# One output piece a block whose low part comes from an accumulating DMA, and eight instead of five blocks a feed-forward sum by all seven products

## The chip, the cores and the metric

The kernel runs on one core of one Trainium2 chip. The core has engines that run side by side, each with its own queue of instructions: TensorE (PE, matmuls; its weight loads are shown as PEld), VectorE (DVE), ScalarE (ACT), GpSimd (POOL) and SyncE (SP). Here SP only issues DMAs; POOL issues DMAs too. The metric is the device time of one execution in microseconds, as the median of several runs. The kernel before took 2389.01 us (three runs, 2388.84 to 2389.03).

## What is computed

One decoder layer in float32, for 256 tokens of width 2048, cut to what matters here:

```python
h = layer_norm(ALPHA * h + 0.5 * swiglu(h, ffn1_w_in, ffn1_w_out), ln1_g, ln1_b)
...
h = layer_norm(ALPHA * h + merged @ w_out, ln2_g, ln2_b)
h = layer_norm(ALPHA * h + 0.5 * swiglu(h, ffn2_w_in, ffn2_w_out), ln3_g, ln3_b)

def swiglu(h, w_in, w_out):
    a, b = split(h @ w_in, 2)
    return (silu(a) * b) @ w_out
```

Between the two feed-forward halves stand attention and a recurrent branch, which form `merged`. The hidden width of a feed-forward half is 5632.

## The kernel before

**Three matmuls for one product.** Each float32 operand is split into a high part, rounded to the format that TensorE streams (`float32r`), and a low part, the rest. A product is high x high + high x low + low x high (`three`, L622 to L625). The weights come from DRAM unsplit, once each, in *pieces* of 128 x 1024 numbers (512 KB), in an order that is fixed while the program is traced (`pieces`, L324 to L380). For each piece ScalarE copies the high part (`wh`, L217) and VectorE subtracts it from the raw weights (`wl`, L218).

**The loop over pieces.** `Weights.unit` (L224) hands TensorE the columns of the current piece, `cur`. At each change of piece it has the loads written down to piece `cur + 8` (AHEAD + LOADS) and the splits to `cur + 4` (AHEAD), and lets every background task go one step (`on_piece`). Plain pieces are loaded to four `raw` buffers; splits have five buffers each for `wh` and `wl` (HL_BUFS).

**Blocks.** The first product of a feed-forward half runs over 22 blocks of 256 hidden columns (a and b, so 512 weight columns). Of a block, the contraction over 2048 is cut into four *chunks* of 512. A chunk is done in one of two ways: as two plain pieces ("c", eight products of the halves of tokens and columns), or by Strassen's scheme with seven products, as four forms of a 1 MB chunk in an `rf` buffer (two such buffers): "p1q3", "p2", "q5p7", "q4p6" (L690 to L704). For the forms VectorE also makes sums of quarters of the weights (`operand`, L182 to L200) before it makes their low parts. Blocks 0 and 1 have no chunk by seven products, block 2 two, later ones three (chunks 1, 2, 3), and the blocks named in FOUR (L96) all four.

**Fills.** Pieces of the second product ("o", output pieces, `fill`, L949) are mixed into the blocks: two in blocks 2 to 5, four in blocks 6 to 21, three of these ahead of the forms and one among them (`block_plan`, L69 to L93). So a three-chunk block has 18 pieces with the last output piece at number 13, counted from 0, and a four-chunk block 20 with the last at number 11. Four output pieces complete 256 tokens x 512 columns for four blocks' hidden columns; the sum goes from PSUM through ScalarE to a `yd` tile and by an accumulating DMA of POOL's to Y (L957 to L961). Y, eight tiles of 128 x 512, is the residual; it is in SBUF during the whole sum. At the end of a block, `gate` (L913) joins the products, applies silu and multiplies.

**After the sums** `out_product` (L871) does the last output pieces, adds the products to Y (`y_add`, L754) and starts the norm, whose power is taken on POOL (L768).

**Buffers and order.** Most tiles of 128 x 512 share the 53 buffers of tag "u" (U_BUFS). A second pool, which `share` (L386) closes and opens again between stages, holds four tiles of forms during the sums ("s") or eight small tiles "t" in the other stages ("t"). The orders of PE, SP and POOL are as the program is written (`manual_schedule`, L293); those of VectorE and ScalarE are made by a planner, which goes by the order of writing and by when it reckons the operands to be there.

## Time and profile before

| | us |
|---|---|
| median of three runs | 2389.01 |
| the profiled execution | 2390.11 |
| its span, first to last instruction | 2388.3 |
| TensorE busy | 2364.0 |
| VectorE busy | 2213.3 |
| ScalarE busy | 1502.0 |
| POOL busy | 123.1 |

The granted TensorE clock was 0.998 of full speed over the span. The profile gives instructions by engine: start, duration, line of the program, operation, output and input tiles with their numbers left out (`wl<-raw,wh`), shapes, and in brackets for how long the engine had been idle before it and what ended that. "DMA to landing" is the time from the issue of a DMA to its last byte. A matmul's duration in the profile is longer than the distance to the next one's start, since matmuls are pipelined; the distance is what counts for time.

The first half runs from the start to about 710 us, of which blocks 0 to 21 to 671, and the second from about 1700 to the end.

### The profile page before, as it was taken

To read this page: it belongs to the slowest core of one execution; us is meant where nothing else is said; L and a number is where in the kernel's file an instruction comes from. 1 tells how busy PE (TensorE), PEld (TensorE's weight loads), DVE (VectorE), ACT (ScalarE), POOL (GpSimd) and SP (SyncE) were. 2 spreads that over 40 slices of the span, in tenths; PEclk is the share of its full clock that TensorE was granted. 3 is DMA by queue.
4 is the path that set the end of the run, shared out by engine and by line. 5 is a ranking of instruction groups with operands and counts; after the bars stand their busy time and mean duration, and the time that the engine had idled before them with its cause. 6 is when DMAs were issued, how large, how long until landed. Compare 5 with 4: busy or idle time off the path is not lost.

```text
span 2388.3 us, 38774 instructions
## 1 busy us (share of the span) xinstructions
PE 2364.0 (99%) x14890; PEld 2111.6 (88%) x14890; DVE 2213.3 (93%) x3127; ACT 1502.0 (63%) x2042; POOL 123.1 (5%) x196
## 2 busy tenths in 40 slices
PE   8999999999999999999999999999999999999997
PEld 6898999989988888888999998888898899899996
DVE  7999999999999998789788888998999999999997
ACT  7666666666647554665588885555766666666662
POOL 0000000000000000001000001100000000000000
PEclk9999999999999999999999999999999999999999
DMA  8666666666666455547655568755675666666665
GB/s 293 193 222 213 227 212 217 219 217 212 195 210 221 177 186 179 187 142 265 207 183 185 187 191 295 252 194 175 209 229 212 221 212 188 230 227 212 216 208 176
DMA packets 123018, 501.24 MB, mean 210 GB/s; under 512 B 14256, under 2 KB 14256, under 8 KB 101968
## 3 DMA queue, kind: packets, MB, share of 16 engines
q1 hardware_dynamic: 104256, 454.60, 54.6%
q0 software_dynamic: 18576, 44.17, 8.1%
q8 instruction: 116, 1.90, 0.3%
q14 instruction: 70, 0.57, 0.1%
HBM read 467.26 MB, written 10.49 MB: 200 GB/s over the span
## 4 chain that ended last, share of the span: by engine, by line
PE 92%; DVE 5%; issue 1%; DMA 1%; ACT 0%; SPq 0%; POOL 0%; DVEq 0%; ACTq 0%; POOLq 0%
PE mm L625 20%; PE mm L623 20%; PE mm L624 20%; PE bp L624 6%; PE bp L623 6%; PE bp L625 6%; PE mm L1248 4%; PE mm L1249 4%; PE mm L1247 4%; DVE wl L218 2%; PE bp L939 1%; DVE ws L190 0%; ACT wh L217 0%; DMA raw<-f1a 0%; PE bp L1128 0%
## 5 line engine op out<-in xcount | busy, mean ns | idle before, releaser
L217 ACT ACTIVATE wh<-raw 128x1024 fp32r<-128x1024 f32 (+2 forms) x540 | 552.3, 1044 | 293.3 <-PE mm L625 169.0
L218 DVE TENSOR_TENSOR wl<-raw,wh 128x1024 fp32r<-128x1024 f32 (+2 forms) x540 | 637.2, 1196 | 96.4 <-ACT wh L217 94.7
L217 ACT ACTIVATE wh<-rf 128x1024 fp32r<-128x1024 f32 (+1 forms) x489 | 439.9, 915 | 313.6 <-PE mm L625 157.3
L218 DVE TENSOR_TENSOR wl<-rf,wh 128x1024 fp32r<-128x1024 f32 (+1 forms) x489 | 505.5, 1040 | 12.8 <-ACT wh L217 7.1
L623 PE MATMUL mm<-wh,hs 128*128 128x512 f32 (+1 forms) x884 | 317.0, 359 | 0.0
L625 PE MATMUL mm<-wh,hs 128*128 128x512 f32 (+1 forms) x884 | 311.1, 352 | 1.1 <-DVE hs L804 1.1
L624 PE MATMUL mm<-wl,hs 128*128 128x512 f32 (+1 forms) x884 | 310.8, 352 | 0.2 <-DVE wl L218 0.2
L625 PE MATMUL mm<-wh,g 128*128 128x512 f32 x704 | 278.2, 395 | 0.2 <-DVE g L747 0.2
L623 PE MATMUL mm<-wh,g 128*128 128x512 f32 x704 | 278.2, 395 | 0.0
L624 PE MATMUL mm<-wl,g 128*128 128x512 f32 x704 | 278.1, 395 | 0.0
L217 ACT ACTIVATE wh<-ws 128x1024 fp32r<-128x1024 f32 x163 | 173.0, 1061 | 141.9 <-PE mm L625 83.9
L623 PE MATMUL bp<-wh,sh 128*128 128x256 f32 x918 | 258.7, 282 | 0.0
L624 PE MATMUL bp<-wl,sh 128*128 128x256 f32 x918 | 256.4, 279 | 1.2 <-DVE wl L218 1.2
L625 PE MATMUL bp<-wh,sl 128*128 128x256 f32 x918 | 256.2, 279 | 0.0
L190 DVE TENSOR_TENSOR ws<-rf 128x1024 f32<-128x1024 f32 x163 | 198.4, 1217 | 7.0 <-DMA rf<-f1a 1.4
L218 DVE TENSOR_TENSOR wl<-ws,wh 128x1024 fp32r<-128x1024 f32 x163 | 198.2, 1216 | 2.8 <-ACT wh L217 2.4
L625 PEld LDWEIGHTS mm<-wh,hs 128*128 128x128 f32 x884 | 165.9, 188 | 27.5 <-DVE hs L804 2.5
L623 PEld LDWEIGHTS mm<-wh,hs 128*128 128x128 f32 x884 | 166.1, 188 | 24.3 <-issue 1.3
L624 PEld LDWEIGHTS mm<-wl,hs 128*128 128x128 f32 x884 | 166.1, 188 | 22.4 <-DVE wl L218 0.7
L1249 PE MATMUL mm<-hs,wl 128*128 128x256 f32 x640 | 179.8, 281 | 0.0
L1247 PE MATMUL mm<-hs,wh 128*128 128x256 f32 x640 | 179.8, 281 | 0.0
L1248 PE MATMUL mm<-hs,wh 128*128 128x256 f32 x640 | 179.8, 281 | 0.0
(312 smaller groups left out, 5291.8 us busy)
## 6 DMA issues: line engine op xcount, KB each, us to landing
rf<-f1a SPq DMA_DIRECT2D x64, 1024.0 KB, 5.4
rf<-f2a SPq DMA_DIRECT2D x64, 1024.0 KB, 5.6
raw<-f1o SPq DMA_DIRECT2D x88, 512.0 KB, 6.5
raw<-f2o SPq DMA_DIRECT2D x88, 512.0 KB, 6.6
raw<-wB SPq DMA_DIRECT2D x80, 512.0 KB, 4.1
raw<-wG SPq DMA_DIRECT2D x54, 512.0 KB, 4.3
raw<-f2a SPq DMA_DIRECT2D x48, 512.0 KB, 4.8
raw<-f1a SPq DMA_DIRECT2D x47, 512.0 KB, 5.3
```

Source lines behind the costliest of these rows:

```text
L190: v.tensor_tensor(t, b[:, 0:4:3], b[:, 1:2].to_broadcast([P, 2, 2, 256]), op=OP.add)
L217: nc.scalar.activation(hp, src, AF.Copy)
L218: self.last = nc.vector.tensor_tensor(lp, src, hp, op=OP.subtract)
L623: T.matmul(ps, xh, w[0], start=start, stop=False)
L624: T.matmul(ps, xh, w[1], start=False, stop=False)
L625: T.matmul(ps, xl, w[0], start=False, stop=stop)
L939: T.transpose(ps[:, k * S + t * P:k * S + (t + 1) * P], z[:, t * 512 + k * P:t * 512 + (k + 1) * P], ident)
L1247: T.matmul(ps[:, :S], w[0], x[:, 0], start=first, stop=False)
L1248: T.matmul(ps[:, :S], w[0], x[:, 1], start=False, stop=False)
L1249: T.matmul(ps[:, :S], w[1], x[:, 0], start=False, stop=last)
```

## The change

- One output piece in each of blocks 6 to 21 (ADDS), the one among the forms, becomes an "O" piece, in the list of pieces "add". `load_to` and `split_to` pass over it. `sum_next`, called at each change of piece, prepares it when it is at most 12 pieces ahead and the last such piece at least 5 behind: SP loads it to a `raw` buffer, ScalarE writes its negated high part to a tile `al` and its high part to `ah` (one buffer each), and POOL issues a DMA that adds the same weights from DRAM to `al`, which leaves the low part there. VectorE has no part in it.
- FOUR has eight blocks instead of five: 7, 9, 11, 13, 15, 17, 19, 21.
- Y lies in DRAM (`acc`) while the feed-forward sums run. `load_x` and `residual` store it there by POOL's DMAs, the accumulating DMAs of `yd` go there, and `fetch_y` brings it back: columns nb 0 and 1 from the background in block 21, 2 and 3 behind that block.
- U_BUFS is 49 instead of 53. `yd` moves to the shared pool, which is now there in all stages, and the tiles that `joined` fills for `product` and for the output of the mixer move from "u" to two buffers "m" of that pool.

```diff
-U_BUFS = 53
+U_BUFS = 49
 Z_BUFS = 1
...
 AHEAD = 4
+ADD_LEAD = 12
+ADD_GAP = 5
 LOADS = 4
...
-FOUR = (9, 12, 15, 18, 21)
+FOUR = (7, 9, 11, 13, 15, 17, 19, 21)
+ADDS = (6, 7, 8, 9, 10, 11, 12, 13, 14, 15, 16, 17, 18, 19, 20, 21)
...
         plans.append(block_plan(FAST if n in FOUR else three, 4, 3))
+        if n in ADDS:
+            i = max(i for i, p in enumerate(plans[n]) if p[0] == "o")
+            plans[n][i] = "O", 0
     return plans
...
 A_ORDER = (6, 7, None, 4, 5, 0, 1, 2, 3)
-assert sum(f == "o" for p in PLANS for f, _ in p) == len(FILLS)
+assert sum(f in "oO" for p in PLANS for f, _ in p) == len(FILLS)
...
         self.pieces = pieces
+        self.adds = deque(i for i, p in enumerate(pieces) if p[1] == "add")
+        self.last_add = -ADD_GAP
         self.raw = {}
...
         ap, form = self.pieces[i]
-        return id(ap) if form else i
+        return id(ap) if form in FORMS else i
...
         ap, form = self.pieces[i]
-        return ap.shape[1] if not form else 512 if form == "p2" else PIECE
+        return ap.shape[1] if form not in FORMS else 512 if form == "p2" else PIECE
...
             k = self.key(self.loaded)
-            if k not in self.raw:
+            if form != "add" and k not in self.raw:
                 n = ap.shape[1]
...
             form = self.pieces[self.split][1]
+            if form == "add":
+                self.split += 1
+                continue
             self.load_to(self.split)
...
+    def sum_next(self):
+        nc = self.nc
+        if self.adds and self.adds[0] <= self.cur + ADD_LEAD and self.cur >= self.last_add + ADD_GAP:
+            i = self.last_add = self.adds.popleft()
+            ap = self.pieces[i][0]
+            t = self.pool.tile([P, PIECE], F32, name=f"raw{i}", tag="raw", bufs=RAW_BUFS)
+            nc.sync.dma_start(t, ap)
+            h, l = (self.pool.tile([P, PIECE], F32R, name=f"a{c}{i}", tag="a" + c, bufs=1) for c in "hl")
+            nc.scalar.activation(l, t, AF.Copy, scale=-1.0)
+            nc.scalar.activation(h, t, AF.Copy)
+            nc.gpsimd.dma_start(l, ap, accum_op=OP.add)
+            self.hl[i] = (h, l)
...
             self.split_to(self.limit or self.cur + AHEAD)
+            self.sum_next()
             self.on_piece()
...
                 pieces.append((ap[:, k * 512:k * 512 + PIECE], None))
-            elif f == "o":
+            elif f in "oO":
                 g, nb, k = next(fills)
                 k += 2 * SEGS[g][0]
-                pieces.append((fo[nb][:, k * 512:k * 512 + PIECE], None))
+                pieces.append((fo[nb][:, k * 512:k * 512 + PIECE], None if f == "o" else "add"))
             else:
...
         p = shared.enter_context(tc.tile_pool(name=name(which), bufs=1))
-        lane[0] = p if which == "t" else None
+        lane[0] = p
         first_home.clear()
...
+    def in_dram(s):
+        return [[spill.tile([P, 512], F32, name=name(s)) for _ in range(4)] for _ in range(2)]
+    acc = [in_dram("ya"), in_dram("yb")]
+    def store(nb, dst):
+        for t in range(2):
+            G.dma_start(dst[t][nb], Y[t][nb])
+    def fetch_y(nb, src):
+        for t in range(2):
+            Y[t][nb] = U("y")
+            G.dma_start(Y[t][nb], src[t][nb])
...
             yield
-        for nb in range(4):
             for t in range(2):
...
                 yield
+            store(nb, acc[0])
...
-    def residual(g, b, away=None):
+    def residual(g, b, away=None, to=None):
         for nb in range(4):
...
             if away:
-                for t in range(2):
-                    Y[t][nb] = U("y")
-                    G.dma_start(Y[t][nb], away[t][nb])
+                fetch_y(nb, away)
             yield
...
                 yield
+            if to:
+                store(nb, to)
...
                 continue
-            if form == "o":
+            if form in "oO":
                 fill()
...
                 if e:
-                    ps = joined(ps, e)
+                    ps = joined(ps, e, M)
                 for t in range(2):
...
-    def ffn(x, forms, ln):
+    def ffn(x, forms, ln, acc):
         def gate(c, e, g, i, lag, plain):
...
+        def later_back():
+            for nb in range(2):
+                yield
+                fetch_y(nb, acc)
...
                 for t in range(2):
-                    u = W.fast_pool.tile([P, 512], F32, name=name("yd"), tag="yd", bufs=2)
+                    u = lane[0].tile([P, 512], F32, name=name("yd"), tag="yd", bufs=2)
                     A.activation(u, open_ps[t], AF.Copy, scale=0.5)
-                    G.dma_start(Y[t][nb], u, accum_op=OP.add)
+                    G.dma_start(acc[t][nb], u, accum_op=OP.add)
...
             for n in range(b0, b1):
+                if n == NBK - 1:
+                    bg.add("back", later_back())
                 c, e = blockF(x, forms, PLANS[n], fill)
...
         new_stats()
+        for nb in (2, 3):
+            fetch_y(nb, acc)
         if not ln.last:
...
-    away = [[spill.tile([P, 512], F32, name=name("ys")) for _ in range(4)] for _ in range(2)]
+    away = in_dram("ys")
...
         for nb in range(4):
-            for t in range(2):
-                G.dma_start(away[t][nb], Y[t][nb])
+            store(nb, away)
     ln = InnerNorm("ln1_g", "ln1_b", FAST_A, put_away)
-    ffn(xs, xf, ln)
+    ffn(xs, xf, ln, acc[0])
     hs = ln.hs
...
-    def joined(c, e):
-        s = [U("stg") for _ in range(2)]
+    def M(s):
+        return lane[0].tile([P, 512], F32, name=name(s), tag="m", bufs=2)
+    def joined(c, e, new=U):
+        s = [new("stg") for _ in range(2)]
         p1, p6, p7, q5 = e[0][:, :S], e[0][:, S:], e[1][:, :S], e[1][:, S:]
...
         c, e = blockF(x, forms, block_plan(fast, 0, 0, len(x) // 4), None)
-        return (joined(c, e), True) if e else (c, False)
+        return (joined(c, e, M), True) if e else (c, False)
...
     new_stats()
-    ln = InnerNorm("ln2_g", "ln2_b", FAST, lambda: bg.add("main", residual(ln2_g, ln2_b)))
+    ln = InnerNorm("ln2_g", "ln2_b", FAST, lambda: bg.add("main", residual(ln2_g, ln2_b, to=acc[1])))
     out_product(mg, ln, mg_forms)
...
-    ffn(ln.hs, ln.forms, OuterNorm(ln3_g, ln3_b))
+    ffn(ln.hs, ln.forms, OuterNorm(ln3_g, ln3_b), acc[1])
```

## The prediction

> **What bounds the kernel now.** I read the page first, then the list of waits of TensorE, then windows over the feed-forward stage. The page's head and its chain that ended last:
>
> ```profile
> span 2388.3 us, 38774 instructions
> PE 2364.0 (99%) x14890; PEld 2111.6 (88%) x14890; DVE 2213.3 (93%) x3127; ACT 1502.0 (63%) x2042; POOL 123.1 (5%) x196
> ...
> PE 92%; DVE 5%; issue 1%; DMA 1%; ACT 0%; SPq 0%; POOL 0%; DVEq 0%; ACTq 0%; POOLq 0%
> ```
>
> TensorE is busy all the time and VectorE nearly so. What TensorE waited for (us in total, times, longest):
>
> ```profile
> PE mm L623 <- ACT wh L217: 7.2, 2, 5.4
> PE bp L624 <- DVE wl L218: 1.2, 2, 0.7
> ```
>
> The first is the start, before any weight is split; the second is all that VectorE's halves (wl) cost it. Now three blocks of the first feed-forward sum, 11, 12 and 13, of which 12 has four chunks by seven products and the others three:
>
> ```profile
> core 0: us, PE busy (x) PEld busy (x) DVE busy (x) ACT busy (x) POOL busy (x), PEclk, DMA share, GB/s
> 321.71:416.86 95.15, 95.15 (x625) 86.37 (x624) 93.39 (x111) 60.91 (x74) 5.25 (x6) 1.00 0.65 216
> ```
>
> Over 95.15 us TensorE never stops, at clock 1.00; VectorE idles 1.76 us, ScalarE 34.2. So the stage is bound by the number of columns that TensorE streams, with VectorE 1.8% behind it. A removed column is time won, as long as VectorE keeps up.
>
> **What a four-chunk block saves.** A chunk by eight products streams 24 matmuls of 512 columns, by seven 42 of 256 (L690 to 704: seven runs of two rows by three). Their pitch, from the starts in the timeline:
>
> ```profile
> 401.28 0.39 PE L623 MATMUL mm<-wh,xs 128*128 128x512 f32 x1
> ...
> 404.07 0.28 PE L623 MATMUL bp<-wh,xs 128*128 128x256 f32 x1
> ...
> 407.58 0.28 PE L623 MATMUL mm<-wh,xs 128*128 128x256 f32 x1
> ```
>
> Twelve of 512 lie between the first two rows, 2.79/12 = 0.2325 us each; thirty of 256 between the last two, 3.51/30 = 0.117. So 5.58 against 4.91 us: 0.67 a chunk. Second way, by ends of blocks, at which ScalarE waits for the last matmul (7 and 8, then 10 and 13):
>
> ```profile
> 226.56 0.38 ACT L920 ACTIVATE z<-bp 128x256 f32<-128x256 f32 x1 [0.33 <-PE bp L625]
> 258.50 0.38 ACT L920 ACTIVATE z<-bp 128x256 f32<-128x256 f32 x1 [0.34 <-PE bp L625]
> ...
> 321.71 0.38 ACT L920 ACTIVATE z<-bp 128x256 f32<-128x256 f32 x1 [0.33 <-PE bp L625]
> 416.86 0.38 ACT L920 ACTIVATE z<-bp 128x256 f32<-128x256 f32 x1 [0.33 <-PE bp L625]
> ```
>
> A three-chunk block takes 31.94. Blocks 11 to 13 take 95.15, so block 12 takes 95.15 - 2 x 31.94 = 31.27, which is 0.67 less. I take 0.67 to 0.70 (a ratio of columns, 1536 of 69632 with the transposes, gives 0.70), 0.685 in the middle. FOUR goes from five blocks to eight: 7, 11, 13, 17, 19 come in, 12 and 18 go out, three more per sum and six in all. **6 x 0.685 = 4.1 us less on TensorE.** Nothing else changes its columns.
>
> **What that costs VectorE, and what the sixteen added pieces give back.**
>
> ```profile
> 376.48 1.22 DVE L190 TENSOR_TENSOR ws<-rf 128x1024 f32<-128x1024 f32 x1
> ...
> 382.99 3.49 DVE L218 TENSOR_TENSOR wl<-raw,wh 128x1024 fp32r<-128x1024 f32 x3
> ...
> 413.55 4.63 DVE L218 TENSOR_TENSOR wl<-raw,wh 128x1024 fp32r<-128x1024 f32 x4 [0.85 <-ACT wh L217]
> ```
>
> From the 376.48 row to the 382.99 row VectorE prepares one seven-product chunk: 6.51 us. A plain piece costs (4.63 - 1.22)/3 = 1.14, a plain chunk two of them, 2.27. The last part of the gate's sum shrinks too (0.68 to 0.41):
>
> ```profile
> L927 DVE TENSOR_TENSOR z<-z,mm 128x512 f32<-128x512 f32 x70 | 45.1, 678 | 0.0
> ...
> L927 DVE TENSOR_TENSOR z<-z,mm 128x256 f32<-128x256 f32 x10 | 4.1, 412 | 0.0
> ```
>
> So a four-chunk block asks 6.51 - 2.27 - 0.27 = 3.97 more of VectorE than a three-chunk one: from 93.39 over three blocks follow 29.8 and 33.8. The second is over TensorE's 31.27, and the four-piece lead (AHEAD) carries it to the next block. After: each of blocks 6 to 21 has one output piece whose low part VectorE doesn't make, 1.14 less. A pair of blocks then asks 63.6 - 2.27 = **61.3 of VectorE in 63.2 of TensorE**: 1.9 idle per pair (0.95 a block) where it was 1.76 per three (0.59). VectorE's cover grows.
>
> **ScalarE** makes two copies of that piece in place of one (l and h in sum_next), both written right behind its load.
>
> ```profile
> 353.94 0.62 ACT L217 ACTIVATE wh<-rf 128x512 fp32r<-128x512 f32 x1
> 356.46 1.06 ACT L217 ACTIVATE wh<-ws 128x1024 fp32r<-128x1024 f32 x1 [1.89 <-PE mm L625]
> 359.31 1.06 ACT L217 ACTIVATE wh<-rf 128x1024 fp32r<-128x1024 f32 x1 [1.79 <-PE mm L625]
> ...
> 390.57 1.06 ACT L217 ACTIVATE wh<-ws 128x1024 fp32r<-128x1024 f32 x1 [2.22 <-PE mm L625]
> ```
>
> Two copies are 2.1 us at most, and at the heads of both kinds of block (353.5 and 384.7) ScalarE has gaps of 1.8 to 2.2 in which it only waits for TensorE to free a buffer. I price them at nothing; if the cover is gone, see the first rival.
>
> **The accumulating DMA.** sum_next runs at a change of piece, at most 12 pieces ahead and 5 behind the last added one: at the first piece of a four-chunk block (added piece is number 11 of 20) and the second of a three-chunk one (13 of 18). The chain in the four-chunk block, read from block 12:
>
> ```profile
> 349.22 0.43 SPq L176 DMA_DIRECT2D raw<-f1o  x1
> DMA to landing us min/median/max: 5.7/6.7/7.6
> ...
> 353.46 0.40 PE L623 MATMUL mm<-wh,g 128*128 128x512 f32 x1
> 372.13 0.39 PE L623 MATMUL mm<-wh,g 128*128 128x512 f32 x1
> ...
> 348.96 1.75 POOL L961 DMA_DIRECT2D y<-yd  x2 [30.17 <-ACT yd L960]
> DMA to landing us min/median/max: 9.3/9.4/9.4
> ...
> DMA to landing us min/median/max: 3.3/7.1/11.4
> ```
>
> SyncE loads this very piece at 349.22 now, behind the same two chunk loads; its place in the queue stays. It lands by 356.8. The low copy ends by 357.9. Before POOL can issue, nothing is queued but yd of the block before, long done; behind POOL's wait for the low copy stands this block's own yd, due only after the piece itself. What 512 KB accumulated from DRAM take, no row shows; nearest are two yd of 256 KB back to back: issued from 348.96, the second 0.7 later, landed 9.4 after its issue, 10.1 in all beside two loads (3.3 to 11.4 over all 80 singles). From below 3.3 + 0.9; from above twice the slowest, 22.8. I take 10.1, for the bytes are the same: landed at 368.0. TensorE reaches the piece at 372.1 less a missing record, about 371.9: **3.9 us spare**, none on the path. In a three-chunk block the piece comes 24.2 us after its start, and 2 us more are spare. The Trainium skill's fit for POOL's DMAs (DMA: Bandwidth & Descriptors, Anatomy of one DMA) is 2.0 us plus bytes over 436 GB/s; by it, an estimate, the 512 KB take 3.2 us and 11 are spare. The yd rows disagree, so the sum goes by them. A rule of it speaks against: on SBUF — State Buffer (Who interferes with whom) a VectorE instruction with two SBUF inputs and a GpSimd one that reads SBUF block one another whole; if each issue held VectorE 0.88, a pair's idle would fall from 1.9 to 0.1. The trace doesn't show it:
>
> ```profile
> 376.08 1.75 POOL L961 DMA_DIRECT2D y<-yd  x2 [25.38 <-ACT yd L960]
> ...
> L961 POOL DMA_DIRECT2D y<-yd x80: 852/878/1215, 77.8 to 2322.6; - x80
> ```
>
> The sums at 376.48 beside it last 1.22 as everywhere.
>
> **DMA engines.**
>
> ```profile
> q1 hardware_dynamic: 3743, 18.87, 54.9%
> q0 software_dynamic: 855, 1.56, 9.7%
> ```
>
> Over 95.15 us six yd took 0.097 x 95.15 = 9.2 us of all engines, 1.54 each. An added piece of twice the bytes is 3.1, or 6.2 per pair: the share rises from 65% to about 75%. Chunk loads have little slack:
>
> ```profile
> 362.95 5.67 SPq L176 DMA_DIRECT2D rf<-f1a  x2
> DMA to landing us min/median/max: 4.8/4.8/4.8
> 368.51 1.22 DVE L190 TENSOR_TENSOR ws<-rf 128x1024 f32<-128x1024 f32 x1
> ```
>
> Issued 362.95, landed 367.75, used 368.51: 0.76 spare. The added DMA runs from about 358 to 368 and may push it by up to 3.1; VectorE would lose 2.3 in a four-chunk block at worst, nothing at best. I take nothing to 1, inside 1.9.
>
> **Residual in DRAM.** 16 stores and 16 fetches of 256 KB per kernel go to POOL (5% busy); x is scaled and stored before the first yd, issued at 77.8. yd then adds into DRAM, off every path until the fetch. The last fetches go out behind block 21 and are wanted twelve output pieces (12 x 2.79, 33 us) later; a fetch of that size took 4.9. The fetch of nb 3 makes POOL wait for block 21's yd to land; behind it comes only the power of the norm (L768), wanted after the whole out product:
>
> ```profile
> y<-ys POOLq DMA_DIRECT2D x8, 256.0 KB, 4.9
> gd<-stg POOLq DMA_DIRECT2D x6, 256.0 KB, 3.5
> ```
>
> U_BUFS 49: during the sums 16 hidden tiles, 12 forms, 12 g and 8 Y are 48 now and 40 after; between them the code holds at most 47, of which two move to "m". A product's "m" pair is free 3.5 after its store, the next comes 21 us later. All at nothing; without cover a late y_add would cost about one fetch, 4.9, per layer.
>
> **Sum.** Profiled execution 2390.11 (span 2388.3 and 1.8 around it), 1.1 over the median of 2389.01; less 4.1 it is 2386.0, and the median **2384.9 us**, 0.17% less. About 0.2%, 4.8 us, is what a measurement tells from no change.
>
> **Rivals.** *VectorE becomes the bound (slower).* The two copies stand in ScalarE's queue behind the load's issue, not its landing. Reached at 354.6, they wait till 355.0 to 356.8 and push the wh of 356.46 to about 359 where VectorE took it at 357.6; in block 13, whose load leaves later, likewise. With a pushed chunk load on top, 1 to 2 us of VectorE per added piece. It decides from 1.9 + 0.26 (4.1 over 16 pairs) = 2.2 a pair, 1.1 a piece, where the kernel is no faster than before. At 2.8 a pair TensorE loses 0.9 x 16 = 14 of VectorE's lateness: 2399; at 3.4, 2409. For it: VectorE at 97%. Against: ScalarE's order is left to the planner, which may put the copies later, and the lead is four pieces.
>
> *The added part comes late.* From 14 us in place of 10.1 TensorE stands at the piece in each of 16 four-chunk blocks; 2 us late is 32 - 4: 2417. The upper bound of 22.8 would be 8.8 late, 2526; it takes two of the slowest end to end, and I leave it out of the range. Against: the slowest yd plus the second half's 1.54 is 12.9.
>
> *Gain not realized.* Where one of the two just passes its point, by 0.26 a pair, the time is that of before, 2389.
>
> *More than the columns.* No row has it: start and transitions hold the other waits. 2384 at most.
>
> **Chances.** Forecast 0.53 (own range 2384.2 to 2387), VectorE 0.23 (2399), late 0.08 (2417), not realized 0.10 (2389), more 0.06. Faster by over 0.2% (under 2384.2): 0.06 and the forecast's lower edge 0.05, 0.11. Slower (over 2393.8): most of the VectorE case, 0.21, and late, 0.08: 0.29. Same: 0.60. Range 2384.0 to 2409: 0.04 below, and above it the worst third of the VectorE case (0.08) and the late one (0.08).
>
> **What would show it.** Right: blocks 7, 9 and so on 31.3 long between L920 rows, the pair 63.2, TensorE's list of waits as short as now, VectorE near 97% in a pair, POOL's new DMAs landing 6 to 12 after issue. Wrong: a wait of mm on the DMA into "al" (late); waits of TensorE on wl, with VectorE's idle put down to ScalarE or to rf (VectorE); a new wait around 690 or 2340 (residual).

## The result, and the profile after

The changed kernel takes **2412.5 us** (median of five runs, 2408.69 to 2415.42) against 2388.84 us of the kernel before on the same chip (2387.06 to 2389.03): 1.010 times as long, interval 1.0086 to 1.0115. It is slower by 23.7 us where 4.1 less had been forecast, and above the range. The profiled execution took 2412.5 us, with a span of 2410.7, which is 22.4 more than before.

The head of the page of the changed kernel and its chain that ended last, then the first lines of TensorE's list of waits (us in total, times, longest):

```profile
span 2410.7 us, 39087 instructions
PE 2373.5 (98%) x14998; PEld 2116.9 (88%) x14998; DVE 2207.1 (92%) x3125; ACT 1526.6 (63%) x2086; POOL 169.2 (7%) x260
...
PE 60%; DVE 9%; issue 2%; ACT 2%; DMA 1%; POOL 0%; DVEq 0%; ACTq 0%; POOLq 0%
```

```profile
PE bp L667 <- DVE wl L232: 9.8, 19, 0.7
PE mm L666 <- ACT wh L231: 6.0, 2, 5.3
PE mm L668 <- DVE g L790: 3.3, 2, 2.0
PE mm L666 <- DVE z L970: 2.7, 3, 1.3
```

The chain is followed back only to 649.80 us, and its shares add up to 74%: TensorE has 60 of these 74 and VectorE 9, against 92 and 5 of 99 before. In the matmuls of the seven products TensorE now stands before VectorE's low parts (wl) nineteen times in place of two. No wait on `al`, the low part that the DMA completes, is in the list. The listed waits of the sums add up to some 13 us more than before, not 22: TensorE's busy time is 9.5 us longer as well (2373.5 against 2364.0), where matmuls follow one another more slowly. So I compare stretches. The windows run from the transposes that end one block's gate, some seven pieces into the block behind it, to those of another: in the kernel before from block 0 to 5 and from 5 to 21 of the first sum, then to block 0 of the second sum, and there from 0 to 5 and from 5 to 21 (called blocks 0 to 4 and 5 to 21 here); then the same in the changed kernel:

```profile
core 0: us, PE busy (x) PEld busy (x) DVE busy (x) ACT busy (x) POOL busy (x), PEclk, DMA share, GB/s
49.89:175.78 125.89, 125.89 (x789) 112.31 (x788) 119.60 (x142) 79.25 (x102) 7.03 (x8) 1.00 0.61 205
175.78:684.19 508.41, 508.41 (x3319) 460.55 (x3317) 497.83 (x607) 324.34 (x395) 28.02 (x32) 1.00 0.66 217
684.19:1709.36 1025.17, 1020.82 (x6379) 907.69 (x6378) 906.63 (x1514) 652.10 (x984) 45.81 (x84) 1.00 0.60 202
1709.36:1836.12 126.76, 126.24 (x789) 112.05 (x788) 125.62 (x162) 78.75 (x102) 7.02 (x8) 1.00 0.62 204
1836.12:2344.72 508.60, 508.60 (x3319) 460.61 (x3317) 496.16 (x583) 323.83 (x394) 28.00 (x32) 1.00 0.66 217
```

```profile
48.99:176.30 127.31, 126.20 (x789) 112.17 (x788) 119.80 (x143) 83.67 (x110) 11.10 (x15) 1.00 0.70 229
176.30:692.16 515.86, 511.84 (x3372) 463.64 (x3371) 493.75 (x604) 334.31 (x415) 45.64 (x55) 1.00 0.75 233
692.16:1719.02 1026.86, 1021.08 (x6379) 907.58 (x6378) 907.91 (x1516) 652.47 (x985) 44.70 (x82) 1.00 0.60 201
1719.02:1850.35 131.33, 127.65 (x789) 111.75 (x788) 125.75 (x162) 80.22 (x104) 13.34 (x19) 1.00 0.70 218
1850.35:2367.57 517.22, 512.53 (x3373) 463.82 (x3372) 492.87 (x582) 335.76 (x414) 45.62 (x55) 1.00 0.75 232
```

| stretch | after less before, us |
|---|---|
| first sum, blocks 5 to 21 | +7.45 |
| second sum, blocks 5 to 21 | +8.62 |
| second sum, blocks 0 to 4 | +4.57 |
| first sum, blocks 0 to 4 | +1.42 |
| between the sums | +1.69 |
| start (-0.90) and end (-0.45) | -1.35 |
| sum | 22.40 |

The granted clock is 1.00 in all of them. In the long stretches, where the forecast was 2.05 less each, 16.1 us were lost; with what should have been gained, 20.2. The first pair of blocks of each long stretch still takes the 63.2 us that were forecast, the third and later ones 64.4 to 65.7. The second place is the start of the second sum.

**The long stretches.** The head of a four-chunk block late in the second sum. ScalarE, VectorE and SP in the timeline (start, duration, and in brackets the idle time before and what ended it):

```profile
2190.11 1.06 ACT L231 ACTIVATE wh<-rf 128x1024 fp32r<-128x1024 f32 x1
2194.35 1.06 ACT L247 ACTIVATE al<-raw 128x1024 fp32r<-128x1024 f32 x1 [3.17 <-DMA raw<-f2o]
2195.32 0.36 ACT L963 ACTIVATE z<-bp 128x256 f32<-128x256 f32 x1
2195.58 0.62 ACT L231 ACTIVATE wh<-rf 128x512 fp32r<-128x512 f32 x1
```

```profile
2195.71 0.42 DVE L964 TENSOR_TENSOR z<-z,bp 128x256 f32<-128x256 f32 x1 [2.17 <-ACT z L963]
```

```profile
2179.80 6.97 SPq L187 DMA_DIRECT2D rf<-f2a  x2
2186.82 0.43 SPq L245 DMA_DIRECT2D raw<-f2o  x1
```

SP issues the raw load of the added piece at 2186.82, after it has been held by the two chunk loads ahead of it (2179.80 to 2186.77). ScalarE comes to the copy `al` at 2191.2, finds the piece not there, and stands for 3.17 us until 2194.35. Behind the copy in its queue are the first step of the gate of the block just ended (L963) and the next chunk's high part; VectorE, which does the gate's next step, stands 2.17 us for the first. A pair of blocks here, from one gate's first step to the next but one, and the same waits over the whole kernel (ScalarE's list, then VectorE's):

```profile
2160.28:2224.93 64.65, 64.09 (x423) 58.00 (x422) 61.76 (x74) 42.05 (x53) 5.25 (x6) 1.00 0.73 228
```

```profile
ACT al L247 <- DMA raw<-f2o: 26.4, 13, 4.1
ACT al L247 <- DMA raw<-f1o: 25.7, 10, 3.7
```

```profile
DVE z L964 <- ACT z L963: 26.6, 12, 3.2
```

VectorE is busy for 61.76 us of the pair, about the 61.3 forecast, but the pair takes 64.65, not 63.2.

**The start of the second sum.** GpSimd's queue there in the changed kernel, then two of VectorE's instructions, then GpSimd's queue before:

```profile
1738.18 0.54 POOL L612 DMA_DIRECT2D yb<-y  x1 [1.19 <-DVE y L649]
1738.72 0.54 POOL L636 DMA_DIRECT2D gr<-ln_g  x1
```

```profile
1734.25 1.29 DVE L647 SCALAR_TENSOR_TENSOR y<-y,gr 128x512 f32<-128x512 f32 x2 [1.98 <-DMA gr<-ln_g]
...
1744.57 0.69 DVE L647 SCALAR_TENSOR_TENSOR y<-y,gr 128x512 f32<-128x512 f32 x1 [2.07 <-DMA gr<-ln_g]
```

```profile
1699.14 0.54 POOL L593 DMA_DIRECT2D gr<-ln_g  x1
```

Before, GpSimd had asked for the last of these rows of the norm's scale at 1699.14. Now the store of a finished part of Y waits in that queue for VectorE (L649), and the rows of the next part stand behind it: the last row of the scale goes out at 1738.72. VectorE needs them and stands 2 us twice, in a stretch in which it had 1.1 us idle in 126.76 before.

### The profile page after: what moved, and what is told of

Same layout as the page of the kernel before. It is cut to its first block, busy times and chain, and to the rows that moved or that the text cites. A ratio compares the mean times of both kernels' runs of the same rounds, so it can differ in the third digit from the quotient of the medians.

```text
span 2410.7 us, 39087 instructions
## 1 busy us (share of the span) xinstructions
PE 2373.5 (98%) x14998; PEld 2116.9 (88%) x14998; DVE 2207.1 (92%) x3125; ACT 1526.6 (63%) x2086; POOL 169.2 (7%) x260
## 4 chain that ended last, share of the span: by engine, by line
PE 60%; DVE 9%; issue 2%; ACT 2%; DMA 1%; POOL 0%; DVEq 0%; ACTq 0%; POOLq 0%
PE mm L666 12%; PE mm L668 12%; PE mm L667 12%; DVE wl L232 4%; PE mm L1302 4%; PE mm L1303 4%; PE mm L1301 4%; PE bp L667 3%; PE bp L668 3%; PE bp L666 3%; ACT wh L231 1%; DVE ws L201 1%; DVE rf L205 1%; DVE rf L208 1%; DVE z L970 0%
## 5 line engine op out<-in xcount | busy, mean ns | idle before, releaser
L231 ACT ACTIVATE wh<-raw 128x1024 fp32r<-128x1024 f32 (+3 forms) x496 | 505.8, 1040 | 247.9 <-PE mm L668 129.8
L232 DVE TENSOR_TENSOR wl<-raw,wh 128x1024 fp32r<-128x1024 f32 (+3 forms) x496 | 584.2, 1194 | 85.9 <-ACT wh L231 83.9
L231 ACT ACTIVATE wh<-rf 128x1024 fp32r<-128x1024 f32 (+1 forms) x507 | 458.2, 914 | 317.7 <-DVE rf L208 175.4
L232 DVE TENSOR_TENSOR wl<-rf,wh 128x1024 fp32r<-128x1024 f32 (+1 forms) x507 | 523.5, 1040 | 13.5 <-ACT wh L231 6.6
L666 PE MATMUL mm<-wh,hs 128*128 128x512 f32 (+1 forms) x872 | 311.3, 357 | 1.4 <-DVE z L970 1.3
L668 PE MATMUL mm<-wh,hs 128*128 128x512 f32 (+1 forms) x872 | 305.1, 350 | 1.1 <-DVE hs L847 1.1
L668 PE MATMUL mm<-wh,g 128*128 128x512 f32 x576 | 227.8, 396 | 3.3 <-DVE g L790 3.3
L666 PE MATMUL mm<-wh,g 128*128 128x512 f32 x576 | 227.7, 395 | 0.0
L667 PE MATMUL mm<-wl,g 128*128 128x512 f32 x576 | 227.5, 395 | 0.0
L232 DVE TENSOR_TENSOR wl<-ws,wh 128x1024 fp32r<-128x1024 f32 x169 | 205.7, 1217 | 8.4 <-ACT wh L231 7.2
L667 PEld LDWEIGHTS bp<-wl,sh 128*128 128x128 f32 x918 | 172.6, 188 | 16.4 <-DVE wl L232 14.4
L1302 PE MATMUL mm<-hs,wh 128*128 128x256 f32 x640 | 179.8, 281 | 0.0
```

Source lines behind the costliest of these rows:

```text
L231: nc.scalar.activation(hp, src, AF.Copy)
L232: self.last = nc.vector.tensor_tensor(lp, src, hp, op=OP.subtract)
L666: T.matmul(ps, xh, w[0], start=start, stop=False)
L667: T.matmul(ps, xh, w[1], start=False, stop=False)
L668: T.matmul(ps, xl, w[0], start=False, stop=stop)
L1302: T.matmul(ps[:, :S], w[0], x[:, 1], start=False, stop=False)
```

## The experiments

Two theories and two rivals were on record. **A**: the copies of the added piece wait in ScalarE's queue for a piece that has not landed and hold what is behind them. **B**: the residual's stores hold the row loads in GpSimd's queue. Rival **F** says that the added pieces cost by being there, wherever they stand. Rival **D** says that VectorE's work in a four-chunk block comes in bursts that the lead of four pieces can't carry, whatever ScalarE does. All times are medians, with the ratio to the kernel before on the same chip and its interval; "over its own before" is the difference from that kernel, 23.7 us for the changed kernel. In the first four runs that kernel took 2387.82 us.

### Copies written nearer to their use (missed)

```diff
-ADD_LEAD = 12
+ADD_LEAD = 9
```

> The lead of the added piece is 9 pieces instead of 12. No other load lies between these places in SyncE's queue, so the load keeps its place and only ScalarE's two copies (and the accumulating DMA) come about three pieces later. Theory A (ScalarE stands at the low copy until the load has landed, 52 us in 23 waits, 3.2 in the four-chunk block from 2195; the gate and the weights' high copies behind it are late, VectorE idles 2.2 and the pair of blocks takes 64.65 instead of 63.2): these waits fall under 10 us in all, a pair takes 63.2 to 63.5, and the time is 2412.5 less 13 to 19 us, 2394 to 2400. Rival D (VectorE's work in a four-chunk block comes in bursts that a lead of four pieces can't carry, whatever ScalarE does): a pair stays above 64.3, the time above 2407.

2410.33 us, 1.0095 (1.008 to 1.011): nearly nothing gained. ScalarE's timeline at the head of the same block shows why:

```profile
2192.31 1.06 ACT L247 ACTIVATE al<-raw 128x1024 fp32r<-128x1024 f32 x1 [3.01 <-DMA raw<-f2o]
2193.28 0.36 ACT L963 ACTIVATE z<-bp 128x256 f32<-128x256 f32 x1
```

The copy again stands ahead of the gate's first step, and waits about as long (3.01 us, 3.17 in the changed kernel). Writing it three pieces later did not move it in ScalarE's queue, whose order the planner makes, and the load kept its place behind the two chunk loads (it goes out at 2184.96). So this run says nothing for or against A: its edit did not change what it was to test.

### The residual's stores behind the row loads

```diff
             gr, br = row(g, nb, "gr"), row(b, nb, "br")
+            if to and nb:
+                store(nb - 1, to)
...
-            if to:
-                store(nb, to)
+        if to:
+            store(3, to)
```

> In residual the store of column block nb to DRAM is issued behind the row loads of nb + 1 instead of ahead of them. Theory B (POOL stands at the store until VectorE has made the column block, the next rows leave late, and VectorE, which is full at the start of the second sum, idles 4.7 us for them): these waits vanish, block 2 of the second sum ends 4 to 4.5 us earlier, the time is 2408. Rival (those blocks are late for another reason, such as the moved tiles): block 2 ends where it did, 2412.

2405.96 us, 1.0073 (1.0057 to 1.009), 6.5 less than the changed kernel, or 5.5 by the times over their own before (18.1 and 23.7). The stretch from block 1 to block 2 of the second sum, in the changed kernel and in this one:

```profile
1736.96:1768.25 31.29, 28.21 (x162) 23.50 (x160) 28.66 (x37) 17.07 (x22) 6.26 (x10) 1.00 0.82 222
```

```profile
1735.80:1762.83 27.03, 27.03 (x161) 23.74 (x160) 26.16 (x33) 17.30 (x22) 4.65 (x6) 1.00 0.76 213
```

It is 4.26 us shorter, with TensorE busy throughout, and the waits on `gr` and `br` are gone. Theory B holds.

### Both edits (missed)

> The edits of e1 and e2 together. Theories A and B: 2389 to 2396, near the kernel before; with nothing else in the way the forecast of 2385 would come back plus about 2 us at the start and end of the first sum. Rival D: above 2402.

2406.05 us, 1.0071 (1.0056 to 1.0086): the time of the rows alone, for the reason given under the first run.

### No added pieces

```diff
-ADDS = (6, 7, 8, 9, 10, 11, 12, 13, 14, 15, 16, 17, 18, 19, 20, 21)
+ADDS = ()
```

> All output pieces are split by VectorE again, as before; the eight four-chunk blocks and the residual in DRAM stay. VectorE's work in a pair of blocks is then 63.6 to 64 us against TensorE's 63.2. Theory A: a pair takes 64.0 to 64.4, less than the 64.65 with the added pieces, for no wait for a load stands in ScalarE's queue; the time is 2402 to 2409. Rival D (the added pieces relieve VectorE as intended and only the bursts cost): a pair takes 65.5 to 66, the time is over 2425.

2402.47 us, 1.0061 (1.0046 to 1.0076). Without the pieces that were to relieve VectorE the kernel is some 9 to 10 us faster than with them. A pair takes 63.9 us between the transposes here, where rival D had put 65.5 to 66: D is refuted. That these blocks without added pieces ask a little more of VectorE than the 63.2 us of TensorE is shown further down (`e11_no_adds_rows`). Still open was what about the added pieces costs the time: their waits or their presence.

### The raw piece earlier in SP's queue

The next four runs, against 2388.04 us of the kernel before.

```diff
-ADD_LEAD = 12
-ADD_GAP = 5
+ADD_LEAD = 14
+ADD_GAP = 2
```

> Edit: the raw piece of each added part is asked for two pieces earlier (ADD_LEAD 14 in place of 12, ADD_GAP 2 in place of 5), so that in SP's queue its load stands ahead of the F1 chunk load that SP waits for, about 6 to 7 us earlier in a four-chunk block, and in ScalarE's queue the gate's first step comes ahead of both copies. Theory A (the copies stand in ScalarE's queue before their piece has landed, and hold the gate's first step and the chunks' high parts; about 1.4 us a pair of blocks and 17 us in all): the 52 us of waits of the copies for DMA all but vanish, the later pairs take 63.2 to 63.5 us in place of 64.4 to 65, time 2394 to 2397. Rival F (the copies cost by being there, 2.1 us of ScalarE and one more load and accumulating DMA in each block, wherever they stand): pairs stay at 64.4 to 65, time 2408 to 2413, with the waits at other instructions.

**2390.69 us, 1.001** (1.0001 to 1.002), 21.8 less than the changed kernel, or 21.0 by the times over their own before (2.7 and 23.7); it is also below the expected 2394 to 2397. The window of the pair that took 64.65:

```profile
2156.44:2219.65 63.21, 63.21 (x425) 57.73 (x424) 61.40 (x74) 42.83 (x53) 5.25 (x6) 1.00 0.76 233
```

TensorE never stops, and the pair takes the forecast's 63.2. The two copies and the accumulating DMA are all still there; rival F falls. The head of the four-chunk block, SP and then ScalarE:

```profile
2163.13 0.43 SPq L245 DMA_DIRECT2D raw<-f2o  x1
2169.31 0.33 SPq L187 DMA_DIRECT2D rf<-f2a  x1
```

```profile
2170.17 1.06 ACT L247 ACTIVATE al<-raw 128x1024 fp32r<-128x1024 f32 x1
...
2175.40 0.37 ACT L963 ACTIVATE z<-bp 128x256 f32<-128x256 f32 x1
```

The load now stands ahead of the second chunk load, for which SP has to wait (2169.31), and the copies are through with no wait 5 us before the gate's first step. The expectation that the waits all but vanish was not met: 18.6 us remain, in 15 waits of at most 1.9, and the pairs are none the longer for them:

```profile
ACT al L247 <- DMA raw<-f2o: 9.6, 8, 1.6
ACT al L247 <- DMA raw<-f1o: 9.0, 7, 1.9
```

### The copies later, the load where it was

```diff
             nc.sync.dma_start(t, ap)
+            self.due = self.cur + ADD_WAIT, i, ap, t
+        if self.due and self.cur == self.due[0]:
+            _, i, ap, t = self.due
+            self.due = None
             h, l = ...
-            nc.scalar.activation(l, t, AF.Copy, scale=-1.0)
-            nc.scalar.activation(h, t, AF.Copy)
+            with self.tc.issue_after(self.last_act.ins):
+                nc.scalar.activation(l, t, AF.Copy, scale=-1.0)
+                nc.scalar.activation(h, t, AF.Copy)
```

ADD_WAIT is 2, and `last_act` the high part split last.

> Edit: the raw piece is asked for where it was; the two copies and the accumulating DMA are written two pieces later, and held behind the high part of the weights split last, so that in ScalarE's queue they come 5 to 7 instructions behind the gate's first step of the block that ended. The loads are those of the changed kernel. Theory A: as with the earlier load, waits of the copies for DMA under 10 us in all, pairs 63.2 to 63.5, 2394 to 2398, unless the accumulating DMA is now late (then TensorE waits on al, which it never did). Rival F: 2408 to 2413.

**2391.0 us, 1.0014** (1.0005 to 1.0024). ScalarE's timeline:

```profile
2176.90 0.38 ACT L971 ACTIVATE z<-bp 128x256 f32<-128x256 f32 x1 [0.34 <-PE bp L676]
...
2183.46 1.05 ACT L254 ACTIVATE al<-raw 128x1024 fp32r<-128x1024 f32 x1
```

The gate's first step waits for TensorE alone, as it did before the change, and the copy 6.6 us behind it finds its piece landed; ScalarE's list has no wait of `al` for a DMA left. The two ways of taking the wait away, from the side of the load and from the side of the queue, give the same time to 0.3 us, again below what was expected. Theory A holds, and had put the loss some 4 us too low. This run also settles the late chunk loads, which the prediction's first rival had put on top of the copies. In the two sums of the changed kernel ScalarE waits for them 12.0 us and VectorE 3.1; here it is 10.3 and 9.5, together more, and the long stretches take 506.37 and 506.90 all the same.

### Both causes taken away

The earlier load and the stores behind the rows together:

> Edit: the earlier load of e7_lead14, and the residual's stores issued behind the row loads of the next part, as in e2_rows_first (which took 6.5 us away). Theories A and B together: the two gains lie in different places and add up, 2387 to 2391, no slower than before. Rival F: 2402 to 2406, as with the rows alone.

2385.83 us, 0.9991 (0.9982 to 1.0001), below the expected 2387 to 2391. And in more rounds, against 2388.25 us of the kernel before, which is also the yardstick of `e10_last_split`, `e11_no_adds_rows` and `e4_five_blocks`:

> Edit: the kernel of e8_lead14_rows again, in more rounds, to tell it from the kernel before. The steady blocks of both sums take 506.35 us each in its trace against 508.41 and 508.60 before, 4.3 us less in all; 1.4 us a sum are lost again in the first five blocks, and 1.3 at the end of the first sum. Theories A and B: 2385 to 2387, 0.05 to 0.13% below the kernel before. Rival: the gain is the spread of the runs, 2388.

**2385.86 us, 0.9987** (0.9978 to 0.9996): faster than the kernel before by 2.4 us, 0.13%. The windows over the long stretches:

```profile
173.24:679.59 506.35, 506.35 (x3373) 461.86 (x3372) 491.71 (x608) 340.61 (x415) 45.65 (x55) 1.00 0.76 237
1832.54:2338.90 506.36, 506.36 (x3373) 461.84 (x3372) 489.93 (x582) 340.31 (x414) 45.67 (x55) 1.00 0.76 238
```

508.41 - 506.35 = 2.06 and 508.60 - 506.36 = 2.24: 4.30 us gained in the two stretches, in which TensorE is busy throughout. Of it 2.4 arrive in the median. The eleven executions lie in two groups, five at 2383.84 to 2384.33 and six at 2385.86 to 2386.28; the profiled one, 2384.06, is of the lower, where the gain is some 4 us.

### The residual in DRAM alone

The five four-chunk blocks of before, and no added pieces:

> Edit: the five four-chunk blocks a layer of before, no added pieces; the residual in DRAM, U_BUFS 49 and the moved tiles stay. Theory B (the residual's stores hold the row loads behind them in the GpSimd queue, in the second sum's first blocks): 2388.8 + 4.2 to 6.5, 2393 to 2395.5, with the interval of 31 us between the first two blocks of the second sum. As I forecast it before (residual in DRAM hidden): 2388 to 2389.

2394.24 us, 1.0025 (1.0016 to 1.0035), against 2388.04: 6.2 us for an edit that was priced at nothing. Theory B's place shows again: from block 1 to block 2 of the second sum it is 31.14 us in its trace, 27.04 before. U_BUFS 49 and the moved tiles are in this run too, and it was not run with the stores behind the rows, so that the stores make up all of the 6.2 is not shown.

### The last added piece left out (not settled)

```diff
-ADDS = (6, ..., 20, 21)
+ADDS = (6, ..., 20)
```

> Edit: as e12_lead14_rows, and the last block of a sum (21) has its low part by VectorE again, not by an added piece. In e8_lead14_rows TensorE waits 1.5 us at the end of the first sum for the gate g of L792, 0.2 before. If that wait comes from the added piece of block 21 (two copies more in ScalarE's queue there), it goes and the time is 2383.5 to 2386; if it comes from the order in which VectorE runs the setup of the next stage, it stays and the time is 2385 to 2387.

2385.88 us, 0.9991 (0.9982 to 1.0): the time of `e12_lead14_rows`. TensorE's wait for `g` at the end of the first sum is 1.0 us here and 1.1 there, so block 21's added piece doesn't set it. Whether the order of VectorE's setup does is not shown.

### Eight blocks without added pieces, stores behind the rows

> Edit: no added pieces (as e5_no_adds) with eight four-chunk blocks, and the residual's stores behind the rows (as e2_rows_first). What the added pieces are worth when they come in time is the difference from e12_lead14_rows. Theory A with VectorE as the limit of a pair (63.9 us a pair measured without them): 2402.5 - 6.5 = 2396, so the pieces are worth 10 us. Rival: they are worth nothing when TensorE bounds, 2386 to 2388.

2397.76 us, 1.0041 (1.0027 to 1.0054). A pair:

```profile
557.93:621.84 63.91, 63.60 (x424) 57.85 (x423) 63.46 (x76) 40.58 (x51) 3.51 (x4) 1.00 0.64 214
```

VectorE is busy 63.46 of 63.91 us: it bounds the pair. So with eight four-chunk blocks the added pieces are needed, and when they come in time they are worth 2397.76 - 2385.86 = 11.9 us.

### Five blocks with added pieces, as written and with the earlier load

```diff
-FOUR = (7, 9, 11, 13, 15, 17, 19, 21)
+FOUR = (9, 12, 15, 18, 21)
```

> Edit: the five four-chunk blocks a layer of before, with the added pieces as the change writes them (ADD_LEAD 12), residual in DRAM. VectorE then has some 3 to 4 us of slack in a triple of blocks. Theory A, in the form that a copy that waits costs only where VectorE has no slack to make up for it: 2394 to 2397, the time of e6_residual_alone. In the form that each wait is paid in full wherever it stands: 2403 to 2411.

2416.64 us, 1.0124 (1.0111 to 1.0138). Neither form of the expectation was met: with slack on VectorE the loss is larger, 28 us. ScalarE's list and timeline, from an execution that took 2422.38:

```profile
ACT al L247 <- DMA raw<-f1o: 53.0, 12, 6.3
ACT al L247 <- DMA raw<-f2o: 47.1, 11, 5.6
```

```profile
2304.26 1.06 ACT L247 ACTIVATE al<-raw 128x1024 fp32r<-128x1024 f32 x1 [4.60 <-DMA raw<-f2o]
2305.23 0.62 ACT L231 ACTIVATE wh<-rf 128x512 fp32r<-128x512 f32 x1
```

The waits are twice as long in all, 100 us, and here a high part of the next chunk stands behind the copy. If that is all, the earlier load takes it away (against 2387.89 us of the kernel before):

> Edit: as e4_five_blocks (five four-chunk blocks a layer, added pieces, residual in DRAM), and the raw pieces asked for two pieces earlier (ADD_LEAD 14, ADD_GAP 2), as in e7_lead14. Theory A without its form 'slack makes up for it': the 28 us of e4_five_blocks over the kernel before are the copies' 100 us of waits for DMA; with the piece landed in time they go, up to the 5 to 6 us of the residual: 2392 to 2396, with 95.15 us a triple of blocks in place of 97.0. Rival: the added pieces cost of themselves where the blocks have three chunks (two copies, a second transfer, wherever they stand): 2405 to 2416.

2394.28 us, 1.0028 (1.0018 to 1.0037). Windows over three blocks at the same place, in `e4_five_blocks` and in this one:

```profile
533.84:631.02 97.18, 96.46 (x627) 86.78 (x626) 90.27 (x107) 62.14 (x78) 7.88 (x9) 1.00 0.72 228
```

```profile
523.76:618.91 95.15, 95.15 (x626) 86.35 (x625) 90.53 (x108) 63.52 (x78) 7.88 (x9) 1.00 0.76 233
```

VectorE does the same work, and the three blocks are back at the 95.15 us of before. The time is that of the residual alone (2394.24): added pieces that come in time cost nothing that these times show, and 2416.64 - 2394.28 = 22.4 us were the wait (22.0 over their own before). In `e7_lead14` it was 21.8, for half the waits. So VectorE's slack did not take the loss away. Whether it is the slack that makes a smaller share of the waits count is not shown, for what stands behind the copies is not the same in the two kernels.

## Why the prediction was wrong, point by point

**What bounds the kernel, and the saving on TensorE**: right. 6 x 0.685 = 4.1 us were forecast, and 4.30 stand in the long stretches of `e12_lead14_rows`; the pair takes 63.2 as forecast. In the changed kernel as it was written, the first pair of each long stretch shows the saving, and the waits of the later ones take more than it gives.

**VectorE's work per pair**: right. 61.3 forecast, 61.4 measured in 63.2 (`e7_lead14`); without the added pieces it is 63.46 and bounds. The slack was worked out rightly, and it was the wrong thing to ask: it covers work, and a late start of the gate or of a high part at best in part, as `e4_five_blocks` shows: with VectorE idle for 6.9 of 97.18 us, the three blocks are 2.0 us longer than before.

**ScalarE's copies, "I price them at nothing": the step that failed.** The forecast compared their 2.1 us with ScalarE's gaps of 1.8 to 2.2 us, which is durations with idle time. What counts is when the operand is there: the piece landed 7.5 us after its issue (2186.82 to 2194.35 with the wait's end), and the copy was reached 4.4 us after it. The term priced at nothing measured 21 to 22 us: 21.8 by `e7_lead14` against the changed kernel, 21.0 over their own before, and 20.4 in the long stretches of the two traces (515.86 and 517.22 against 506.36 each). The prediction's row for this load was of block 12, where it left SP at 349.22 and ScalarE's gap began at 354.6, which gave waits of 0.4 to 2.2; measured are 52.1 us in 23 waits, up to 4.1.

**The rival named it.** "VectorE becomes the bound" put the copies in ScalarE's queue "behind the load's issue, not its landing", at 2399 to 2409, with a chance of 0.23. The copies waiting for their piece and holding what is behind them is right, and so is the size for them alone: `e2_rows_first`, in which only this cost is left, takes 2405.96. Its sign came too, TensorE's waits on wl with VectorE idle for ScalarE (26.6 us in 12 waits). The rival named the high parts behind the copies; in the block shown it is the gate's first step that VectorE stands for. What its name says is not right: VectorE is idle 2.9 us of 64.65 in the pair above, and is late rather than full. Against the rival the prediction had set that the planner may put the copies later. It put them ahead of the gate's first step; the profile of before has no such copies, so it could not tell that.

**Residual in DRAM, "all at nothing": the second step that failed.** The forecast counted the DMAs' issue on GpSimd, 5% busy, and the fetches at the end. It followed yd's and the fetch's place in that queue, and not that of the stores in `residual`, which wait for VectorE with the next row loads behind them. Price: 4.26 us in the one stretch, 4.9 to 5.5 by the times of kernels with and without, over their own before (`e7_lead14` to `e8_lead14_rows`, and the changed kernel to `e2_rows_first`); the whole move to DRAM, alone, 6.2. No rival held it, and it takes the time from the rival's 2405 to above the range.

**The accumulating DMA**: off the path, as forecast. Its tile in the changed kernel:

```profile
L249 POOL DMA_DIRECT2D al<-f1o x16: 872/872/875, 171.4 to 649.8; - x16
...
DMA to landing us min/median/max: 5.2/5.5/6.0
```

10.1 us were taken from the yd rows, and here 512 KB from DRAM landed in 5.5 (median). It is not one number: in `e7_lead14` the same DMAs took 5.8 to 9.5 (median 7.6), in `e9_copies_behind` 7.4 to 10.4 (8.6), so the forecast's 10.1 lies near the slowest. TensorE never waits for it in any of the three, and "the added part comes late" is refuted. The fit in the Trainium skill (DMA: Bandwidth & Descriptors, Anatomy of one DMA) gave an estimate of 3.2, below all of these. The rule weighed from the Trainium skill (SBUF — State Buffer, Who interferes with whom), taken as if each of GpSimd's issues held VectorE, shows nowhere in the time: six issues stand in the pair of 63.21 us in which TensorE never stops, and VectorE is busy 61.40 of it where 61.3 had been worked out.

**DMA engines**: right; 65% to 75% forecast, 0.76 in the pair. Chunk loads: not the cause, by `e9_copies_behind`, where they are waited for as long and the long stretches are short again.

**U_BUFS 49, "m" and the moved tiles**: no cost shows. From the first sum's end to the second's start it is 1.69 us more in the changed kernel, and 1.8 of TensorE's wait for `g` at the end of the first sum (2.0 after, 0.2 before) lie in that stretch. In the trace of `e5_no_adds`, which has these edits too, it is 0.09 less than before.

**What adds up.** With both causes taken away the 23.7 us over its own before become 2.2 less (`e8_lead14_rows`). Taken one after the other, the copies' wait is 21.0 and the stores 4.9; in the other order the stores are 5.5 and the copies 20.3. So the two costs hardly depend on one another. What stays open are 1.9 us of the 4.3 between the long stretches and the median of `e12_lead14_rows`. In the trace of `e8_lead14_rows` blocks 0 to 4 take 1.35 and 1.40 us more than before, in that of `e12_lead14_rows` 0.10 less and 0.41 more, so that it differs between executions of one kernel. A late chunk load fits: in the late blocks of `e8_lead14_rows` VectorE waits 1.5 us for one at 104.39 and ScalarE 1.3 at 1784.87, and in `e12_lead14_rows` neither waits there. What makes it late is not shown. The wait for `g` at the end of the first sum, 1.5 and 1.1 us in these traces against 0.2 before, is another part.

## What to carry to other kernels

An instruction added to an in-order queue is priced by when its operand is there, not by its duration: find what stands behind it and how late that may be, above all if a planner sets the place. Spare time on the engine that waits next didn't pay for such a wait here, for it is the start that comes late. And a store put into a queue holds every load written behind it: issue the next loads first.

## What the runs showed of the hardware that I had not expected

- Moving a load two pieces up in SP's queue was worth 21 to 22 us: it no longer stands behind a load that SP has to wait for, 7 us in the block shown, and it also lands sooner after its issue (median 5.1 us in `e7_lead14`, 7.4 in the changed kernel).
- An accumulating DMA of 512 KB from DRAM landed in 5.2 to 6.0 us in the changed kernel (plain loads of the same weights and size: median 7.0), but in 5.8 to 9.5 in `e7_lead14` (plain loads 6.5). Its median was 5.5, 7.6 and 8.6 us in three kernels that move the same bytes.
- The place that the planner gives the copies depends on the blocks: with five four-chunk blocks they waited 100 us in all, with eight 52, in 23 waits each.
